# S5 output tables on SyncE's queue, and the squares of the z gates' norm in a ring of their own

## The chip, the cores and the metric

The kernel runs on one core of a Trainium2 chip. The metric is the device time of one execution in microseconds, the median of several. Engine names in the rows: PE is TensorE's matmuls, PEld its weight loads, DVE is VectorE, ACT is ScalarE, POOL is GpSimd, SP is SyncE. A name with a q behind it (SPq, ACTq) is that engine's sequencer, where transfers are issued.

## What is computed

One inference step of a decoder with two layers, for 512 prompt tokens and 64 sample tokens (576 columns together), all in fp32. Each layer has a token mixer with three branches on the same input, then a channel mixer.

```python
gates, u, q, k, v, fg, z, xbc, dt_raw = jnp.split(h @ p['w_in'][l], _in_split_points(), axis=-1)
...
y_s5, s5_re, s5_im = s5_branch(u, ...)
...
    y_fox = fox_prompt(q, k, v, logf)
...
y_ssd, conv_new, ssd_new = ssd_branch(z, xbc, dt_raw, ...)
merged = (gates[:, :, 0] * (y_s5 @ p['w_branch_s5'][l])
          + gates[:, :, 1] * (y_fox @ p['w_branch_fox'][l])
          + gates[:, :, 2] * (y_ssd @ p['w_branch_ssd'][l]))
out = merged @ p['w_o'][l]
```

The S5 branch is a complex diagonal state-space scan whose output goes through a gelu and a gated linear unit (GLU). FoX is an attention with forget gates. SSD is a chunked state-space scan whose output is multiplied by silu(z) and divided by its root mean square:

```python
y = y.reshape(bsz, seq, SSD_WIDTH) * jax.nn.silu(z.astype(jnp.float32))
y = y * lax.rsqrt(jnp.mean(jnp.square(y), axis=-1, keepdims=True) + RMS_EPS) * norm_w.astype(jnp.float32)
```

The channel mixer is a dense SwiGLU in layer 0 and a top-2-of-8 expert SwiGLU in layer 1.

## The kernel before, in words

Activations lie with channels on partitions and the 576 tokens in the free dimension, in two halves of 288. A dense projection goes by blocks of 128 output columns. `wload` (line 265) loads one block of weights, 512 KB, through SP's queue into a tile wr (three buffers). `wsplit` makes two parts of it, a rounded high part on ACT (line 97) and the rest on DVE (line 106), into wh and wl (four buffers each, two to a block of eight k-tiles). `mm3` (lines 294 to 296) then makes three matmuls for each of eight k-tiles and two halves: 48 to a block. Two PSUM banks (tag mm) hold the halves.

The order of the work: the kernel is written under a scheduler that orders each engine's instructions by a simulated time, with earlier written work first, and gives buffers out as they come free. SP is taken out of this (`manual_schedule` for SP): its queue is issued in the order in which the program is written.

`mixer(l)` is written in this order: the convolution and SSD's inputs (`conv`), `ssd`, `kqv_fox`, `s5_scan_and_out`, `fox_sample`, `fillers`, `s5_glu`, one z block, `merge5`. `kqv_fox` loads and multiplies twelve blocks (k, q and v for four pairs of heads, evacuated at line 850) and runs the prompt attention in small steps: scores (line 907), a softmax (lines 908 to 915), transposes (line 232) and the product with v (line 930). `fillers` are dense blocks with no tie to the branches: eight gate blocks in either layer (line 1337) and three z blocks (line 1344).

`s5_scan_and_out(l)` multiplies the inputs by tables (line 549), scans along time with small DVE products (lines 100, 103, 106 with tiles V and st), and swaps halves (tile vx). Its last loop goes over four groups q. For each it loads tables from DRAM: eight transfers tu of 64 KB (line 621) and a cu, in four transfers for odd q (line 627) or two for even q (line 632). All are issued by ACT. tu and the odd cu take the tag T, with three buffers in the mixer's phase, which `ssd_sample` uses for the four state tiles h0s (loaded at line 1147, stored at line 1315). The even cu takes the tag A. Lines 641 and 642 multiply tu by the inputs uc and cu by the scanned states, and the result yg passes a gelu, goes through DRAM (YD) and becomes the GLU's input.

`gate_z` is called in `merge` after its first block. It multiplies y by silu(z), squares each of four tiles on ACT (line 1258), adds them up on POOL (line 1260 and the helper at line 103), sums over partitions with a matmul by ones (line 1263), and takes the root and the reciprocal (rs, lines 1265 and 1266). Squares and rs take the tag SQ, three buffers in the phase of the mixer's end. In layer 0 that tag also holds halves of spilled gates, loaded from GD at line 1386; line 1382 loads the S5 part of the merge through POOL's queue. The work ring h288 (four buffers of one half) exists throughout, and holds z and GLU tiles in the mixer and selection tiles in routing.

Of the kernel before, what the change touches and what calls it, by code (L numbers as in the profile page):

```python
# [8 lines left out]
F32 = mybir.dt.float32  # L9
# [10 lines left out]
P = 128  # L20
# [4 lines left out]
HF = T // 2  # L25
# [20 lines left out]
def decoder_step(ctx, tc, A, O):  # L46
    nc = tc.nc
    act, dve, pool, pe, sp = nc.scalar, nc.vector, nc.gpsimd, nc.tensor, nc.sync
    consts = ctx.enter_context(tc.tile_pool(name="consts", bufs=1))
    wk = ctx.enter_context(tc.tile_pool(name="wk", bufs=2))  # L50
# [9 lines left out]
    def U(tag, shape, dt=F32, name="u"):  # L60
        return cur["pool"].tile(shape, dt, name=name, tag=tag, bufs=cur["bufs"][tag])

    def UA(shape, dt=F32, name="u"):
        return U("A", shape, dt, name)
# [19 lines left out]
    def PX(name="px"):  # L84
        return ps.tile([P, 512], F32, name=name, tag="px", bufs=2)
# [7 lines left out]
    def P5(name="p5"):  # L93
        return ps.tile([P, 512], F32, name=name, tag="p5", bufs=1)

    def cp(out, in_):
        return act.activation(out, in_, AF.Copy)  # L97

    def mul(e, out, a, b):
        return e.tensor_tensor(out, a, b, op=OP.mult)  # L100

    def add(e, out, a, b):
        e.tensor_tensor(out, a, b, op=OP.add)  # L103
# [4 lines left out]
    def stt(out, a, s, b, op0, op1):  # L108
        dve.scalar_tensor_tensor(out, a, s, b, op0=op0, op1=op1)  # L109
# [410 lines left out]
    def s5_scan_and_out(l):  # L520
# [97 lines left out]
        for q in range(4):  # L618
            tus = U("T", [P, 8, P], name="tu")
            for s in range(8):  # L620
                act.dma_start(out=tus[s * 16:(s + 1) * 16],
                              in_=KZ[l][q, :, (1 + s) * 16:(1 + s) * 16 + P].rearrange("(g c) t -> c g t", c=16))
            if q % 2:
                cu = U("T", [P, 8, P], name="cu").rearrange("p (a g) t -> p a g t", a=2)
                for i in range(2):
                    for a in range(2):
                        act.dma_start(out=cu[i * 64:i * 64 + 64, a],
                                      in_=CD[l][a * 64:a * 64 + 64, i, q * 4:q * 4 + 4, 16:144])
            else:
                cu = UA([P, 2, 4, 144], name="cu")  # L630
                for i in range(2):
                    act.dma_start(out=cu[i * 64:i * 64 + 64],
                                  in_=CD[l][:, i, q * 4:q * 4 + 4].rearrange("(a n) g t -> n a g t", a=2))
                cu = cu[:, :, :, 16:144]
            for a in range(2):
                tu = tus[:, a:8:2]
                pt = P5()
                pv = pt[:, :288].rearrange("p (g k) -> p g k", g=4)
                for g in range(4):
                    gp = q * 4 + g  # L640
                    pe.matmul(pv[:, g, :], lhsT=tu[:, g, :], rhs=uc[a][:, gp, :], start=True, stop=False)
                    pe.matmul(pv[:, g, :], lhsT=cu[:, a, g], rhs=vs[a][:, gp, 0:72], start=False, stop=True)
                yv = yg[a][:, q * 4:q * 4 + 4, :]
                y2v = [wk.tile([P, HF], F32, name="ygl", tag="v288", bufs=4).rearrange("p (g k) -> p g k", g=4)
                       for i in range(2)]
                cp(yv, pv)
                mul(dve, y2v[0], yv, yv)
                dve.tensor_scalar(y2v[0], y2v[0], 0.044715, 1.0, op0=OP.mult, op1=OP.add)
                mul(dve, y2v[0], y2v[0], yv)
                act.activation(y2v[1], y2v[0], AF.Tanh, scale=math.sqrt(2.0 / math.pi))  # L650
                stt(yv, y2v[1], 1.0, yv, OP.add, OP.mult)
# [39 lines left out]
    def YV(h, l_):  # L691
        return (V2(h), V2(l_))
# [54 lines left out]
    def mixer(l):  # L747
# [62 lines left out]
        ssd(l)  # L810
        kqv_fox(l, w_in)
        sg = s5_scan_and_out(l)
        fox_sample(l)
        fillers(l)
# [426 lines left out]
    def gate_z(l, w_in):  # L1241
        pr = prm[l]
        y2 = [U("M", [P, 2, T], name=f"y2{i}") for i in range(2)]
        zs = [U("M", [P, 2, T], name=f"zs{i}") for i in range(2)]
        for j in range(4):
            pool.dma_start(out=y2[j // 2][:, j % 2], in_=YS[l][j])
        for j in range(4):
            pool.dma_start(out=zs[j // 2][:, j % 2], in_=ZD[l][j])
        yh = [U("C", [P, 2, T], F32R, name=f"ysh{i}") for i in range(2)]
        yl = [U("C", [P, 2, T], F32R, name=f"ysl{i}") for i in range(2)]  # L1250
        for h in range(2):
            pt = PX()
            s2 = U("L", [P, HF], F32, name="lns2")
            for j in range(4):
                y_ = y2[j // 2][:, j % 2, HS[h]]
                mul(dve, y_, y_, zs[j // 2][:, j % 2, HS[h]])
                sq = U("SQ", [P, HF], F32, name="sq")
                act.activation(sq, y_, AF.Square)
                if j == 0:
                    pool.tensor_copy(s2, sq)  # L1260
                else:
                    add(pool, s2, s2, sq)
            pe.matmul(pt[:, :HF], lhsT=ones, rhs=s2, start=True, stop=True)
            rs = U("SQ", [P, HF], F32, name="rs")
            act.activation(rs, pt[:, :HF], AF.Sqrt, scale=0.25 / 512, bias=eps[:, 0:1])
            dve.reciprocal(rs, rs)
            for j in range(4):
                y_ = y2[j // 2][:, j % 2, HS[h]]
                mul(dve, y_, y_, rs)
                nw = pr[:, R_NW + j:R_NW + j + 1]  # L1270
                act.activation(yh[j // 2][:, j % 2, HS[h]], y_, AF.Copy, scale=nw)
                stt(yl[j // 2][:, j % 2, HS[h]], y_, nw, yh[j // 2][:, j % 2, HS[h]].bitcast(F32), OP.mult, OP.subtract)
        return YV(yh, yl)
# [95 lines left out]
    def merge(l, yf, mhl):  # L1369
# [10 lines left out]
        def front(j):  # L1380
            m5 = wk.tile([P, T], F32, name="m5", tag="xp", bufs=4)
            pool.dma_start(out=m5, in_=MD[l][j])
            if 1 in SPILL[l]:
                t = gtile(("XS", "SQ"))
                for h in range(2):
                    pool.dma_start(out=t[h], in_=GD[l][8 + j, :, HS[h]])
            else:
                gates(GLEAD)
                t = ready.pop((1, j))
            t = gated(l, 1, j, yf, t)  # L1390
            if j == 0:
                with tc.issue_after(S["mm"].ins):
                    ys.append(gate_z(l, A["w_in"][l]))
            for h in range(2):
                add(dve, m5[:, HS[h]], m5[:, HS[h]], t[h])
            return m5
# [641 lines left out]
```

## Time and profile before

| | us |
|---|---|
| median of 3 runs | 2404.74 |
| lowest and highest | 2397.31, 2407.87 |
| the profiled execution: its own time | 2400.34 |
| the profiled execution: span from first to last instruction | 2398.7 |
| mean granted TensorE clock over the span (1 is full) | 0.968 |

The rows further down come from the profiled execution. A row of a group of instructions gives the line, the engine, the operation, output and inputs by their names in the program, the shapes, the count, the busy time and the mean of one, and the idle time ahead of them with what ended it. Matmuls are pipelined, so their busy times overlap; how fast they really follow each other is read from their count in a stretch.

### The profile page before, as it was taken

How to read it: one execution, taken by the hardware profiler on the slowest of the kernel's cores; microseconds unless marked ns; L12 is line 12 of the kernel's file. 1: busy time of each engine (PE TensorE's matmuls, PEld its weight loads, DVE VectorE, ACT ScalarE, POOL GpSimd, SP SyncE). 2: the span in 40 equal slices, each digit the busy share in tenths (PEclk: the TensorE clock that was granted, in tenths of full speed). 3: DMA queues.
4: the chain of work that ended last, by engine and by line, in shares of the span. 5: the costliest groups of instructions: out<-in, count | busy, mean ns of one | idle time of the engine just before them, and what ended most of it. 6: DMA issues, size and time to landing. Idle time of an engine off the chain costs nothing. (4 is left out here: it accounts for less than half of the span.)

```text
span 2398.7 us, 45369 instructions
## 1 busy us (share of the span) xinstructions
PE 2277.4 (95%) x17037; PEld 2158.2 (90%) x17038; DVE 1573.7 (66%) x3725; ACT 1134.5 (47%) x2538; POOL 560.4 (23%) x712
## 2 busy tenths in 40 slices
PE   5999999998999999999999999899999699999995
PEld 5899997888998999999899998789999599999995
DVE  4956687556588843334765697456447578888886
ACT  2354443453346323223644443354334467777773
POOL 6733224333130110001124324233003310101000
PEclk7999999999999999999999999899999799999997
DMA  5566556856445432233576557757333799999993
GB/s 125 174 177 206 160 155 186 202 160 215 118 126 157 147 96 83 80 89 103 139 188 184 157 152 195 186 156 211 89 99 108 199 229 255 255 253 259 236 258 100
DMA packets 587436, 399.91 MB, mean 167 GB/s; under 512 B 59436, under 2 KB 548188, under 8 KB 587176
## 3 DMA queue, kind: packets, MB, share of 16 engines
q1 hardware_dynamic: 475272, 236.30, 37.2%
q0 software_dynamic: 30912, 95.12, 14.4%
q10 hardware_dynamic: 81024, 65.51, 9.5%
q8 instruction: 136, 2.23, 0.4%
q14 instruction: 92, 0.75, 0.1%
HBM read 326.02 MB, written 70.92 MB: 165 GB/s over the span
## 5 line engine op out<-in xcount | busy, mean ns | idle before, releaser
L106 DVE TENSOR_TENSOR wl<-wr,wh 128x512 fp32r<-128x512 f32 x886 | 629.1, 719 | 364.0 <-ACT wh L97 346.6
L97 ACT ACTIVATE wh<-wr 128x512 fp32r<-128x512 f32 x886 | 549.0, 625 | 511.0 <-PE mm L295 364.9
L294 PE MATMUL mm<-xh,wh 128*128 128x288 f32 (+1 forms) x2048 | 617.8, 302 | 15.3 <-issue 7.9
L295 PE MATMUL mm<-xl,wh 128*128 128x288 f32 (+1 forms) x2048 | 613.9, 300 | 7.9 <-issue 5.2
L296 PE MATMUL mm<-xh,wl 128*128 128x288 f32 (+1 forms) x2048 | 612.8, 299 | 5.1 <-issue 4.4
L294 PEld LDWEIGHTS mm<-xh,wh 128*128 128x128 f32 (+1 forms) x2048 | 386.3, 189 | 26.0 <-issue 11.6
L295 PEld LDWEIGHTS mm<-xl,wh 128*128 128x128 f32 (+1 forms) x2048 | 386.1, 189 | 17.1 <-issue 10.9
L296 PEld LDWEIGHTS mm<-xh,wl 128*128 128x128 f32 (+1 forms) x2048 | 385.8, 188 | 13.1 <-issue 9.8
L1788 PE MATMUL mm<-xe,wh 128*128 128x352 f32 x448 | 134.3, 360 | 1.8 <-issue 1.8
L1788 PE MATMUL pf<-xe,wh 128*128 128x352 f32 x448 | 132.2, 358 | 0.5 <-issue 0.5
L1789 PE MATMUL mm<-xe,wl 128*128 128x176 f32 x512 | 118.0, 251 | 1.8 <-issue 1.8
L1789 PE MATMUL pf<-xe,wl 128*128 128x176 f32 x512 | 117.6, 250 | 1.5 <-issue 1.5
L294 PE MATMUL mm<-hq,wh 128*128 128x288 f32 x352 | 104.3, 296 | 0.2 <-DVE rf L103 0.2
L294 PE MATMUL pf<-xh,wh 128*128 128x288 f32 x352 | 104.3, 296 | 0.0
L296 PE MATMUL mm<-hq,wl 128*128 128x288 f32 x352 | 104.2, 296 | 0.0
L296 PE MATMUL pf<-xh,wl 128*128 128x288 f32 x352 | 104.1, 296 | 0.0
L295 PE MATMUL pf<-xl,wh 128*128 128x288 f32 x352 | 103.8, 295 | 0.0
L295 PE MATMUL mm<-hq,wh 128*128 128x288 f32 x352 | 103.7, 295 | 0.0
L1789 PEld LDWEIGHTS mm<-xe,wl 128*128 128x128 f32 x512 | 97.9, 194 | 1.6 <-issue 1.6
L1789 PEld LDWEIGHTS pf<-xe,wl 128*128 128x128 f32 x512 | 97.2, 193 | 0.5 <-issue 0.5
L1788 PEld LDWEIGHTS mm<-xe,wh 128*128 128x128 f32 x448 | 86.5, 193 | 2.4 <-issue 2.4
L1337 ACT ACTIVATE gt<-mm,prm 128x288 f32<-128x288 f32 x96 | 47.4, 494 | 85.4 <-PE mm L296 75.1
(662 smaller groups left out, 5310.4 us busy)
## 6 DMA issues: line engine op xcount, KB each, us to landing
wr<-in_w_in_dram SPq DMA_DIRECT2D x108, 512.0 KB
wr<-in_moe_w_gate_dram SPq DMA_DIRECT2D x64, 512.0 KB
wr<-in_moe_w_up_dram SPq DMA_DIRECT2D x64, 512.0 KB
wr<-in_moe_w_down_dram SPq DMA_DIRECT2D x64, 512.0 KB
wr<-in_w_o_dram SPq DMA_DIRECT2D x32, 512.0 KB
wr<-in_ffn_w_gate_dram SPq DMA_DIRECT2D x25, 512.0 KB
wr<-in_ffn_w_up_dram SPq DMA_DIRECT2D x25, 512.0 KB
wr<-in_ffn_w_down_dram SPq DMA_DIRECT2D x24, 448.0 KB
```

The source lines that it names most:

```text
L97: return act.activation(out, in_, AF.Copy)
L106: e.tensor_tensor(out, a, b, op=OP.subtract)
L294: pe.matmul(o, lhsT=wh_[:, a, :m], rhs=x[0][:, k, s], start=(st and k == 0), stop=False)
L295: pe.matmul(o, lhsT=wh_[:, a, :m], rhs=x[1][:, k, s], start=False, stop=False)
L296: S["mm"] = pe.matmul(o, lhsT=wl_[:, a, :m], rhs=x[0][:, k, s], start=False, stop=(sp_ and k == kt - 1))
L1337: act.activation(t[h], o[h], AF.Tanh, scale=0.5, bias=prm[l][:, c0:c0 + 1])
L1788: pe.matmul(o, lhsT=h_[:, k % 4, :], rhs=xf, start=(k == 0), stop=False)
L1789: pe.matmul(o[:, 0:CAP], lhsT=l_[:, k % 4, :], rhs=x[:, k, 0], start=False, stop=False, skip_group_check=True)
```

## The change

The table loads of `s5_scan_and_out` are issued by SP in place of ACT, at the same place in the program. In `gate_z`, the squares and rs take buffers of the ring h288 in place of the tag SQ.

```diff
@@ -618,18 +618,18 @@
         for q in range(4):
             tus = U("T", [P, 8, P], name="tu")
             for s in range(8):
-                act.dma_start(out=tus[s * 16:(s + 1) * 16],
+                sp.dma_start(out=tus[s * 16:(s + 1) * 16],
                               in_=KZ[l][q, :, (1 + s) * 16:(1 + s) * 16 + P].rearrange("(g c) t -> c g t", c=16))
             if q % 2:
                 cu = U("T", [P, 8, P], name="cu").rearrange("p (a g) t -> p a g t", a=2)
                 for i in range(2):
                     for a in range(2):
-                        act.dma_start(out=cu[i * 64:i * 64 + 64, a],
+                        sp.dma_start(out=cu[i * 64:i * 64 + 64, a],
                                       in_=CD[l][a * 64:a * 64 + 64, i, q * 4:q * 4 + 4, 16:144])
             else:
                 cu = UA([P, 2, 4, 144], name="cu")
                 for i in range(2):
-                    act.dma_start(out=cu[i * 64:i * 64 + 64],
+                    sp.dma_start(out=cu[i * 64:i * 64 + 64],
                                   in_=CD[l][:, i, q * 4:q * 4 + 4].rearrange("(a n) g t -> n a g t", a=2))
                 cu = cu[:, :, :, 16:144]
@@ -1254,14 +1254,14 @@
             for j in range(4):
                 y_ = y2[j // 2][:, j % 2, HS[h]]
                 mul(dve, y_, y_, zs[j // 2][:, j % 2, HS[h]])
-                sq = U("SQ", [P, HF], F32, name="sq")
+                sq = wk.tile([P, HF], F32, name="sq", tag="h288", bufs=4)
                 act.activation(sq, y_, AF.Square)
                 if j == 0:
                     pool.tensor_copy(s2, sq)
                 else:
                     add(pool, s2, s2, sq)
             pe.matmul(pt[:, :HF], lhsT=ones, rhs=s2, start=True, stop=True)
-            rs = U("SQ", [P, HF], F32, name="rs")
+            rs = wk.tile([P, HF], F32, name="rs", tag="h288", bufs=4)
             act.activation(rs, pt[:, :HF], AF.Sqrt, scale=0.25 / 512, bias=eps[:, 0:1])
```

## Rows read from the trace of the kernel before

**Rows 1.** The page's busy times: us, share of the span, instructions.
```profile
PE 2277.4 (95%) x17037; PEld 2158.2 (90%) x17038; DVE 1573.7 (66%) x3725; ACT 1134.5 (47%) x2538; POOL 560.4 (23%) x712
```
**Rows 2.** Line 265 on SP's queue, 260 to 380 and 1340 to 1460; timeline between.
```profile
L265 SPq DMA_DIRECT2D wr<-in_w_in_dram x11: 367/368/368, 265.6 to 378.3; - x11
...
393.81 61.63 SPq L265 DMA_DIRECT2D wr<-in_s_w_glu_dram  x4
...
L265 SPq DMA_DIRECT2D wr<-in_w_in_dram x11: 367/368/368, 1343.3 to 1454.9; - x11
```
**Rows 3.** Lines 621 and 627: durations (ns min/median/max), first and last start; both layers.
```profile
L621 ACTq DMA_DIRECT2D tu<-KZ x32: 309/430/1690, 396.7 to 446.3; - x32
...
L627 ACTq DMA_DIRECT2D cu<-CD x8: 580/602/664, 420.6 to 450.4; - x8
...
L621 ACTq DMA_DIRECT2D tu<-KZ x32: 309/328/1545, 1477.9 to 1526.3; - x32
...
L627 ACTq DMA_DIRECT2D cu<-CD x8: 582/616/920, 1500.7 to 1531.0; - x8
```
**Rows 4.** Tile kq on ACT, 300 to 320 and 1375 to 1392 us.
```profile
L850 ACT ACTIVATE kq<-mm x2: 411/412/412, 305.2 to 310.8; 128x288 f32<-128x288 f32 x2
...
L850 ACT ACTIVATE kq<-mm x3: 393/410/410, 1377.9 to 1388.6; 128x288 f32<-128x288 f32 x3
```
**Rows 5.** Groups by line on PE, 311 to 450 and 1389 to 1531 us.
```profile
L294 PE MATMUL mm<-xh,wh 128*128 128x288 f32 x154 | 47.3, 307 | 0.0
...
L294 PE MATMUL mm<-xh,wh 128*128 128x288 f32 x152 | 46.2, 304 | 0.0
```
**Rows 6.** Stretches: us, busy of PE, PEld, DVE, ACT, POOL (count), clock, DMA, GB/s.
```profile
320.00:388.00 68.00, 67.88 (x474) 59.33 (x472) 67.47 (x241) 27.15 (x64) 18.57 (x25) 1.00 0.54 154
388.00:450.00 62.00, 55.42 (x360) 45.73 (x359) 31.16 (x80) 20.05 (x54) 20.56 (x31) 0.92 0.87 208
1400.00:1460.00 60.00, 60.00 (x432) 54.09 (x431) 59.02 (x215) 25.34 (x61) 15.99 (x22) 1.00 0.52 138
1460.00:1531.00 71.00, 67.69 (x428) 56.65 (x427) 38.88 (x101) 24.36 (x65) 23.59 (x35) 0.90 0.78 193
```
**Rows 7.** The same view for tile mm alone: PE, PEld, DVE, ACT.
```profile
388.00:450.00 62.00, 23.81 (x132) 19.67 (x131) 0.82 (x2) 2.23 (x5) 0.92 0.87 208
540.00:560.00 20.00, 20.00 (x153) 20.00 (x152) 4.54 (x10) 0.00 (x0) 1.00 0.83 250
...
1460.00:1531.00 71.00, 22.89 (x144) 19.53 (x143) 0.46 (x1) 2.40 (x5) 0.90 0.78 193
```
**Rows 8.** Groups by line on DVE, 320 to 388 us.
```profile
L100 DVE TENSOR_TENSOR st<-a,V 128x112 f32<-128x112 f32 (+1 forms) x54 | 18.6, 369 | 0.1
L106 DVE TENSOR_TENSOR wl<-wr,wh 128x512 fp32r<-128x512 f32 x12 | 8.2, 683 | 0.0
```
**Rows 9.** Stores of h0s; from the timelines, a tu issue and its first matmul.
```profile
L1315 ACTq DMA_DIRECT2D out_dram<-h0s x4: 396/401/401, 380.3 to 418.2; - x4
...
402.37 0.31 ACTq L621 DMA_DIRECT2D tu<-KZ  x1
...
408.38 0.41 PE L641 MATMUL p<-uc,tu 128*128 128x72 f32 x2 [3.09 <-DMA out_dram<-h0s]
```
**Rows 10.** Groups by line on PE, 450 to 500 us: FoX after the last table.
```profile
L930 PE MATMUL pf<-pT,vt 128*64 128x128 f32 x36 | 5.4, 282 | 0.8 <-ACT pT L97 0.8
...
L232 PE MATMUL pf<-ident,s 128*128 128x128 f32 x20 | 3.6, 278 | 0.4 <-DVE s L109 0.4
```
**Rows 11.** Timelines of ACT and POOL in `gate_z` of layer 0; PE's waits, 560 to 600.
```profile
569.40 0.44 ACT L1258 ACTIVATE sq<-y 128x288 f32<-128x288 f32 x1
...
575.76 0.43 ACT L1258 ACTIVATE sq<-y 128x288 f32<-128x288 f32 x1
...
575.57 0.54 POOL L1382 DMA_DIRECT2D m<-MD  x1 [7.04 <-DVE yfl L106]
...
PE px L1263 <- POOL lns L103: 4.1, 1, 4.1
```

## The prediction

> **What bounds the kernel now.** I read the page first: TensorE is busy for 95% of the span and no other engine for more than 66% [rows 1]. So a change pays or costs by the idle time that it takes from TensorE or gives it. Next I asked what the edited lines stand beside. The table loads of lines 621, 627 and 632 lie in the second half of each mixer, so I read SP's queue there. In layer 0 it issues eleven w_in loads between 265.6 and 378.3 us, then four for the S5 GLU; in layer 1 eleven between 1343.3 and 1454.9 us [rows 2]. By the program these are the eight gate blocks and three z blocks of `fillers`, in exactly the order in which they are written: SP's queue is issued in program order, since only SP is under the manual schedule. The ACT queue is not: its table loads, written ahead of `fillers`, run from 396.7 to 450.4 us in layer 0 and from 1477.9 to 1531.0 us in layer 1, long after the filler loads have gone out [rows 2, 3].
>
> Then I asked what TensorE lives on. The copies of the last V block end k, q and v at about 311 us in layer 0 and 1389 us in layer 1 [rows 4]. From there to the last table load, line 294 issues 154 and 152 matmuls [rows 5]; lines 295 and 296 belong to the same products, so some 462 and 456 in all. In a stretch with nothing else, 153 of them take 20 us, 0.131 us each [rows 7]. So 60.5 and 59.7 us of TensorE's work there is filler. The rest is three chains of small steps: SSD, FoX and the S5 scan. They cannot run ahead at will: from 320 to 388 us VectorE is busy 67.47 of 68 us and from 1400 to 1460 us 59.02 of 60, most of it the scan's small products (line 100 alone 18.6 us) [rows 6, 8].
>
> **The first edit: tables on SP.** Each layer issues 32 tu loads and 12 cu loads. They leave ACT and stand in SP's queue where the program has them: behind the last load of `kqv_fox` and ahead of the eleven filler loads. Nothing is computed differently. What changes is who stands behind a wait. tu and the odd cu take the tag T, three buffers that the SSD's h0s hold; these are stored from 380.3 to 418.2 us [rows 9], and only then do the first slots come free. Even with all three slots free, the tu of q = 2 takes the buffer of q = 0, which line 641 reads only after the scan; its first matmul starts at 408.38 us [rows 9]. So SP must stand still until the third and fourth groups can be issued, and behind it wait the fillers, then the GLU loads, the last z block and the w_branch loads. ACT's splits wait for these loads, and TensorE for the splits.
>
> The terms, for both layers:
> - **Cover lost.** No filler matmul can run before the last table is issued: 60.5 + 59.7 = 120.2 us of work that today lies under the chains moves behind them.
> - **Chains faster.** Without fillers the chains have the engines to themselves. In the stretch that VectorE bounds, the splits of fillers go: 12 of line 106, 8.2 us in layer 0 [rows 8], and I take the same for layer 1. In the second stretch, 388 to 450 us, fillers take 132 x 0.131 = 17.3 us and TensorE idles 62 - 55.42 = 6.6 us; in layer 1 144 x 0.131 = 18.9 and 71 - 67.69 = 3.3 us [rows 6, 7]. Chains made of waits get only part of that back: bounds nothing and all, 23.9 and 22.2 us; I take half, since ACT also loses its table issues (32 x 0.430 + 12 x 0.602 = 21 us in layer 0, 32 x 0.328 + 12 x 0.616 = 18 us in layer 1 [rows 3]). Together -(8.2 + 11.9) - (8.2 + 11.1) = -39.4 us; bounds 0 and -62.5.
> - **Work pulled forward.** FoX steps that today run after the last table can fill the hole: 5.4 + 3.6 = 9.0 us in layer 0 after 450 us [rows 10], the same taken for layer 1: -18 us; bounds 0 and -18.
> - **Restart.** When SP is free, TensorE waits for the first load and its split: from a last tu issue at 402.37 to its matmul at 408.38 us are 6.0 us [rows 9], and a split adds one pass of VectorE (0.68 us [rows 8]) and about as much of ACT: 7.3 us, twice, 14.6 us.
> - **Clock.** In the second stretches the granted clock already stands at 0.92 and 0.90 [rows 6], a mix of the 2.4 GHz and the 1.2 GHz level, where TensorE works in pieces. That is worth 0.08 x 62 + 0.10 x 71 = 12.1 us today. Without fillers the work is sparser, so I add as much again: +12.1. No row shows such a hole, so the bounds are wide: 0, and half of the other matmuls' time there (62 - 6.6 - 17.3 = 38.1 and 71 - 3.3 - 18.9 = 48.8 us), 44 us.
>
> **The second edit: a ring for the squares.** In `gate_z` of layer 0 the tag SQ (three buffers) also holds gate halves loaded from GD. The second square ends near 569.8 us, the third starts at 575.76; meanwhile POOL, which adds them up, stood 7.04 us in a load at line 1382 [rows 11]. TensorE waits 4.1 us for that sum at line 1263 [rows 11]. With four buffers of h288, unused in this phase until routing, the squares run ahead and the sum of the second half is ready sooner. POOL's stall stays. I take -5 us for both layers; bounds -10 (the clock's recovery with it) and 0, as no new wait can come from buffers that are free.
>
> **Sum.** 120.2 - 39.4 - 18.0 + 14.6 + 12.1 - 5.0 = +84.5 us on the profiled execution's own 2400.34 us, which is 0.2% under the median of 2404.74: 2485 us, 3.5% slower. All bounds at their best give 120.2 - 62.5 - 18.0 + 14.6 - 10 = +44 us, 2445; all at their worst 120.2 + 14.6 + 44 = +179 us, 2579.
>
> **Rule against row.** The rows show that the moved loads change place against the weight loads, not only their issuer [rows 2, 3]; the sum goes by that. The Trainium skill, "DMA: Bandwidth & Descriptors", section "Issuing engines are not separate DMA queues", says that loads started from sync, scalar or gpsimd share the same 16 DMA engines and that another issuer only saves the sequencer's issue time. By that rule alone the move would be worth ACT's issue time and no more, the third rival below.
>
> **Rivals.**
> *SP is not held (faster).* If SP's queue could pass the table loads, fillers would still start at 265 us, and the tables would land without ACT's delays. TensorE's idle time in the second stretches would go (6.6 + 3.3 us), with the clock's 12.1 us and the ring's 5: 2400.3 - 27 = 2373 us. It decides if the tables' buffers are free before the last k, q, v block is used up, at 311 and 1389 us. Against it: the eleven loads in written order [rows 2], h0s stored only from 380.3 us on and line 641 at 408.38 [rows 9]. Chance 0.08.
> *The chains close up (no change).* If SSD, FoX and scan without fillers ran as fast as TensorE can take them, the hole would hold little idle time, and restart less ring would be left: +14.6 - 5.0, 2410 us. For it: TensorE has 72 us of other work there (139 - 60.5 - 6.6). Against: VectorE's full 68 us, of which fillers make only 8.2 [rows 6, 8]. Chance 0.05.
> *Only issue time moves (no change).* ACT is busy 20.05 of 62 us in the second stretch [rows 6], so freeing its queue is worth at most TensorE's idle time there, 6.6 + 3.3 us, and the ring 5: 2385 us or, where ACT was not the cause, 2400. It is what the Trainium skill's rule above gives. Chance 0.03.
>
> **How the numbers follow.** A measurement of this kernel can tell about 0.5% from no change, 12 us. The forecast, SP held by the tables, has the remaining 0.84. Slower takes that and 0.01 of the closed-up chains that end just beyond the mark; the other rivals split: 0.08 for faster, 0.07 for the same. The range runs from 2430, where chains close up further than my best bounds (more of FoX's sample part pulled forward), to 2555, short of all bounds at their worst at once. What lies outside are the rivals and some 0.04 on top.
>
> **What would show it.** In the changed kernel SP's queue should show 44 table issues between the last k, q, v load and the first filler load, and filler loads starting near 430 and 1510 us of chain time instead of 265 and 1343. TensorE's idle time should lie between the last V copy and the first gate copy, some 35 to 45 us a layer, with waits that end at a split or at chain steps, and a lower granted clock there. ACT should lose the issues of lines 621 to 632. If filler loads still start before the tables, the first edit was mis-read; if the hole is there but TensorE stays over 90% busy in it, the chains closed up; if line 1263 still waits 4 us, the ring did nothing.

## Result and profile after

The changed kernel takes 2490.36 us (median of 4 runs, 2488.98 to 2492.37), the kernel before 2402.34 us beside it (4 runs): ratio 1.037, 95% interval 1.0349 to 1.0391. The forecast was 2485 us, slower. The profiled execution took 2490.47 us, its span is 2488.8 us at a mean granted clock of 0.951, against 2398.7 us at 0.968.

First the page's busy times, which answer [rows 1]: the same number of matmuls, but 34.7 us more of TensorE's time, and a smaller share of a longer span.

```profile
PE 2312.1 (93%) x17037; PEld 2177.2 (87%) x17038; DVE 1570.7 (63%) x3725; ACT 1139.7 (46%) x2538; POOL 549.6 (22%) x712
```

The timeline of SP's queue (start, us, engine, line, operation, tile, count) from 240 to 520 us answers [rows 2, 3].

```profile
249.90 9.08 SPq L265 DMA_DIRECT2D wr<-in_w_in_dram  x2
385.40 3.66 SPq L621 DMA_DIRECT2D tu<-KZ  x8
...
449.09 2.56 SPq L627 DMA_DIRECT2D cu<-CD  x4
451.75 62.02 SPq L265 DMA_DIRECT2D wr<-in_w_in_dram  x9
```

And SP's waits from 240 to 700 us (total, times, longest):

```profile
SPq L621 <- DMA out_dram<-h0s: 130.2, 3, 126.3
SPq L621 <- PE p L642: 25.1, 2, 23.0
```

SP issues the last k, q, v loads by 259 us (249.90 + 9.08) and then stands in one wait of 126.3 us for the store of h0s, whose buffer the first tu takes. Later it stands 23.0 us for the matmuls of line 642 that read an earlier group's tables. The first filler load goes out at 451.75 us; before, the eleven went out from 265.6 us on [rows 2].

What TensorE gets from that is in the stretch between the last v copy and the last table, which answers [rows 5 to 7]. The first row is the kernel before, 311 to 450 us, the second the changed kernel over the same 139 us, both with all tiles (columns as in [rows 6]); the third is tile mm alone in the changed kernel, 320 to 460 us.

```profile
311.00:450.00 139.00, 132.30 (x922) 113.20 (x921) 104.44 (x335) 52.54 (x133) 43.72 (x63) 0.96 0.71 180
...
312.00:451.00 139.00, 103.50 (x567) 72.70 (x565) 101.11 (x346) 46.23 (x129) 47.61 (x69) 0.78 0.54 139
...
320.00:460.00 140.00, 0.00 (x0) 0.00 (x0) 0.00 (x0) 0.00 (x0) 0.78 0.56 145
```

No filler matmul for 140 us, TensorE busy for 103.5 us instead of 132.3, and a granted clock of 0.78 instead of 0.96. The clock is a mix of the 2.4 GHz and the 1.2 GHz level. The chains are no shorter for it: the last table is issued at 451.0 us, against 450.4 [rows 3].

To see where the 90 us came in, I cut both traces near the same events: shortly after the start of FoX in each mixer (its first score matmul, line 907, starts at 245.8 and 1323.1 us before, at 246.8 and 1374.3 us after), and at the first (layer 0) or last (layer 1) matmul of line 1263. Before:

```profile
250.00:583.00 333.00, 323.59 (x2540) 286.57 (x2539) 218.38 (x591) 146.78 (x356) 107.33 (x152) 0.98 0.68 187
583.00:1330.00 747.00, 730.16 (x5439) 714.20 (x5438) 443.94 (x972) 304.43 (x622) 112.50 (x153) 0.98 0.44 125
1330.00:1676.50 346.50, 333.99 (x2570) 296.65 (x2569) 223.42 (x583) 154.25 (x367) 115.20 (x155) 0.97 0.65 178
```

After:

```profile
250.00:642.70 392.70, 348.81 (x2570) 302.56 (x2569) 224.04 (x601) 149.62 (x357) 107.05 (x158) 0.92 0.58 162
642.70:1380.00 737.30, 723.11 (x5408) 707.62 (x5407) 439.66 (x963) 304.16 (x620) 109.31 (x146) 0.99 0.44 125
1380.00:1768.00 388.00, 351.12 (x2579) 306.75 (x2578) 225.42 (x587) 156.27 (x367) 113.14 (x157) 0.90 0.59 160
```

Layer 0's mixer is 59.7 us longer, layer 1's 41.5; the middle is 9.7 and the rest 1.4 us shorter: 90.1 in all. Of the 59.7, 34.5 are idle time of TensorE (392.7 - 348.81 against 333 - 323.59) and 25.2 longer busy time for nearly the same matmuls (30 more of 2540); of the 41.5, 24.4 and 17.1. So of 101.2 us in the two mixers 58.9 are idleness; 42.3 are matmuls that take longer, by the lower clock or by standing apart in the pipeline, which the busy time does not tell apart. Cut exactly from line 907's first matmul to line 1263's first, the two mixers are 58.9 and 39.5 us longer, with again 59 us of idle time and 39 us of busy time.

The ring did move a wait. TensorE's waits from 560 to 670 us in the changed kernel, against [rows 11]:

```profile
PE mm L294 <- ACT ysh L1271: 5.6, 2, 4.0
...
633.68 0.54 POOL L1382 DMA_DIRECT2D m<-MD  x1 [7.61 <-DVE yfl L106]
```

Line 1263 no longer waits for POOL's sum. The next matmuls, which read the product ysh, wait for 5.6 us in its place, and POOL stands 7.61 us ahead of a load of line 1382, for the tile yfl, as before (7.04 us). (The second line is from POOL's timeline.)

### The profile page after: what moved, and what is told of

It is laid out like the page before. It is cut to its first block, busy times and chain, and to the rows that moved or that the text cites. A ratio compares the mean times of both kernels' runs of the same rounds, so it can differ in the third digit from the quotient of the medians.

```text
span 2488.8 us, 45500 instructions
## 1 busy us (share of the span) xinstructions
PE 2312.1 (93%) x17037; PEld 2177.2 (87%) x17038; DVE 1570.7 (63%) x3725; ACT 1139.7 (46%) x2538; POOL 549.6 (22%) x712
## 5 line engine op out<-in xcount | busy, mean ns | idle before, releaser
L295 PEld LDWEIGHTS mm<-xl,wh 128*128 128x128 f32 (+1 forms) x2048 | 386.6, 189 | 14.6 <-issue 9.0
L1788 PEld LDWEIGHTS pf<-xe,wh 128*128 128x128 f32 x448 | 85.5, 191 | 2.4 <-issue 2.4
## 6 DMA issues: line engine op xcount, KB each, us to landing
wr<-in_ffn_w_down_dram SPq DMA_DIRECT2D x24, 448.0 KB
```

Of the source, the lines that this page charges most:

```text
L295: pe.matmul(o, lhsT=wh_[:, a, :m], rhs=x[1][:, k, s], start=False, stop=False)
L1788: pe.matmul(o, lhsT=h_[:, k % 4, :], rhs=xf, start=(k == 0), stop=False)
```

## Experiments

My theory: a table load that waits for a buffer stands at the head of SP's queue, and the filler loads behind it leave the chains of the mixer without cover. I call the stretch without fillers the hole. Rivals: ACT losing the table issues is what costs; the number of loads is; of the hole, only TensorE's idle time could take up work, or none of it. Kernels measured together share runs of the kernel before on the same chip, where it took 2379 to 2383 us. The ranges in us of the first four expectations were worked out from the 2402 us of the result; they are compared by ratio.

**The tables alone.** The changed kernel, with sq and rs back in tag SQ.

```diff
-                sq = wk.tile([P, HF], F32, name="sq", tag="h288", bufs=4)
+                sq = U("SQ", [P, HF], F32, name="sq")
-            rs = wk.tile([P, HF], F32, name="rs", tag="h288", bufs=4)
+            rs = U("SQ", [P, HF], F32, name="rs")
```

> The first edit alone: table loads on SP, squares back in SQ. My theory (SP held by the tables takes the fillers' cover): all of the loss is here, 2490 to 2497 us, that is the changed kernel plus the ring's 0 to 5 us. Rival (a good part of the loss comes from the ring, whose h288 buffers or changed order delay the end of the mixer): below 2470 us.

2456.91 us against 2379.34: ratio 1.0296 (1.0247 to 1.0345). This missed my range, which is 1.036 to 1.039 as a ratio. Still, most of the loss is the tables', 78 of the 85 to 88 us that the whole change costs. The wait of line 1263 is back:

```profile
PE px L1263 <- POOL lns L103: 4.5, 1, 4.5
```

**The ring alone.** The kernel before, with the second edit only.

```diff
-                sq = U("SQ", [P, HF], F32, name="sq")
+                sq = wk.tile([P, HF], F32, name="sq", tag="h288", bufs=4)
-            rs = U("SQ", [P, HF], F32, name="rs")
+            rs = wk.tile([P, HF], F32, name="rs", tag="h288", bufs=4)
```

> The second edit alone: tables on ACT as before, squares and rs in h288. My theory: 2397 us, 5 us under the kernel before, and TensorE's wait for POOL's sum at line 1263 (4.1 us in layer 0) gone. Rival (POOL's queue sets the sum, not the buffers): no change within 0.2%, and the wait only moves to the next reader of the norm.

2380.15 us against 2379.34: ratio 0.9994 (0.9969 to 1.0018). No difference that can be told; the interval, 7 us less to 4 us more, does not exclude the 5 us of the forecast. TensorE's waits from 540 to 670 us:

```profile
PE mm L294 <- ACT ysh L1271: 5.3, 2, 4.0
```

The wait of line 1263 is gone and 5.3 us stand at line 294: what was ready sooner was not what comes last. Whether the ring costs anything together with the moved tables stays open: the whole change gave 1.0351 and 1.0364 further down, tables alone 1.0296, with intervals that overlap.

**Filler loads first.** The changed kernel, with the loads of all eleven filler blocks written ahead of the tables, on the same queue.

```diff
-        sg = s5_scan_and_out(l)
+        s5h = s5_scan_and_out(l)
+        next(s5h)
+        cols = [br_ * 1024 + j * P for br_ in SPILL[l] for j in range(8 if l or br_ else 0)] + \
+            [C_Z + j * P for j in range(4 - NZ[l])]
+        PRE.extend(wload(w_in, c, P, 8) for c in cols[:11])
+        sg = next(s5h)
...
-                w = wsplit(wload(src, c0 + j * P, P, kt), P, kt)
+                w = wsplit(PRE.pop(0) if PRE else wload(src, c0 + j * P, P, kt), P, kt)
```

(s5_scan_and_out yields once ahead of its last loop.)

> The changed kernel, with the eleven filler loads of each layer put ahead of the table loads in SP's queue; tables still on SP, ring kept, the same work. My theory (place in SP's queue is the whole cost): the hole after k, q, v closes, filler matmuls run from about 311 us, and the time is 2385 to 2415 us, about that of the kernel before. Rival (the cost is in what ACT gives up or in how SP issues 44 small loads): 2470 to 2495 us, like the changed kernel.

2368.87 us against 2379.34: ratio 0.9952 (0.9925 to 0.9979). SP's timeline:

```profile
240.65 121.31 SPq L265 DMA_DIRECT2D wr<-in_w_in_dram  x12
378.56 7.42 SPq L623 DMA_DIRECT2D tu<-KZ  x8
...
431.44 2.56 SPq L629 DMA_DIRECT2D cu<-CD  x4
434.10 7.30 SPq L265 DMA_DIRECT2D wr<-in_s_w_glu_dram  x4
```

The same 44 loads on the same queue, and the whole loss is gone; between 320 and 340 us tile mm has 99 matmuls again. So it is the order on the queue. This kernel is slightly faster than the kernel before, by about half a per cent; which part of it makes that gain was not separated.

**The last group alone.** Only the twelve loads of q = 3 on SP, the ring kept.

```diff
-                act.dma_start(out=tus[s * 16:(s + 1) * 16],
+                (act if q < 3 else sp).dma_start(out=tus[s * 16:(s + 1) * 16],
```

(and so at lines 627 and 632)

> Ring kept; of the four groups of tables only the last (q = 3, 12 of 44 loads) goes through SP, the others through ACT as before. My theory (the last table's wait decides when SP comes free, not the number of loads): nearly the whole loss, 2470 to 2495 us. Rival (the loss grows with the loads moved): 12/44 of 88 us, about 2425 us.

2464.4 us: ratio 1.0347 (1.03 to 1.0395). A quarter of the loads costs what all of them cost. SP's timeline:

```profile
231.89 9.08 SPq L265 DMA_DIRECT2D wr<-in_w_in_dram  x2
419.56 6.80 SPq L621 DMA_DIRECT2D tu<-KZ  x8
426.59 2.60 SPq L627 DMA_DIRECT2D cu<-CD  x4
429.30 89.61 SPq L265 DMA_DIRECT2D wr<-in_w_in_dram  x11
```

**The first group alone.** The same with `act if q else sp`: ten loads, whose buffers come free first.

> Only the eleven... no: only the ten table loads of the first group (eight tu, two cu of q = 0) are issued by SP; the other 34 stay on ACT, and the ring of the squares is kept. Theory (fillers are held until SP's last table load is out, and what they lose is the cover between the last k, q, v block and that time): SP comes free once the state stores give the first buffers back, near 395 to 400 us instead of 430 to 450, so filler matmuls are still missing for most of the chains' time (from 311 to about 400 us and in layer 1 from 1389 to about 1490 us); work covered again is the filler work of the last 50 us of each chain stretch, some 15 to 20 us a layer. Ratio 1.010 to 1.028, the first filler load near 400 us. Rival (the price comes from the later groups, whose buffers wait for the scan's reads): ratio 1.000 to 1.005.

2468.82 us against 2382.52: ratio 1.0348 (1.0297 to 1.0399). This missed my range: SP was free 50 us earlier than in the changed kernel, and the loss stayed. SP's timeline, then ACT's and TensorE's in layer 1:

```profile
364.89 3.67 SPq L621 DMA_DIRECT2D tu<-KZ  x8
380.25 1.31 SPq L632 DMA_DIRECT2D cu<-CD  x2
381.66 107.97 SPq L265 DMA_DIRECT2D wr<-in_w_in_dram  x11
...
1513.23 6.94 ACTq L621 DMA_DIRECT2D tu<-KZ  x1
...
1520.92 5.06 ACTq L621 DMA_DIRECT2D tu<-KZ  x2
1526.03 0.63 ACT L97 ACTIVATE wh<-wr 128x512 fp32r<-128x512 f32 x1 [5.00 <-DMA tu<-KZ]
...
1526.71 0.61 PE L294 MATMUL mm<-xh,wh 128*128 128x288 f32 x1 [15.58 <-ACT wh L97]
```

Less came back in either layer than I had forecast. In layer 0 the first matmul of line 1263 comes at 617.4 us, against 626.5 in the changed kernel beside it: 9 us came back, not 15 to 20, since the fillers now fall on the chains' last steps (the last S5 matmul, of line 642, moves from 448.0 to 462.2 us). In layer 1 the filler loads go out together with ACT's tables, one table issue takes 6.94 us where the median was 0.328 [rows 3], and a split behind them holds TensorE for 15.58 us; from FoX's first score to line 1263 that mixer is 2.2 us shorter than in the changed kernel. The profiled execution then loses 11.7 us behind line 1263 of layer 1, which no row explains; 10 us is also about what the interval leaves open. I read from it that the cover that counts lies before 390 us, where the scan fills VectorE, and that what SP can load after that is late already; no run tests this by itself.

**Four fillers first.** As "filler loads first", with `cols[:4]`.

> The changed kernel, with the loads of the first four filler blocks of each layer written ahead of the table loads on SP (three raw buffers stand ahead, so the fourth load waits for a split). Theory (each filler block whose load gets past the tables gives back its 48 matmuls x 0.131 us = 6.3 us of cover): four blocks a layer give back 25 us a layer, 50 of the about 85 to 92 us: ratio 1.012 to 1.022. Rival (any block behind the tables keeps the loss, since the chains then still end in an idle stretch and at a lower clock): ratio over 1.025. Rival (a few blocks are enough, because the rest of the hole has other work): ratio under 1.008.

2424.06 us: ratio 1.017 (1.0124 to 1.0216). Against the changed kernel beside it (2467.3) 43 us came back, where four blocks a layer make 50. This fits a cost that goes by the blocks whose loads come too late, each worth about its matmuls' time.

**Tables on POOL's queue.** `pool.dma_start` at lines 621, 627 and 632 of the changed kernel.

> The changed kernel with the 44 table loads of each layer on POOL's queue in place of SP's; POOL's order is the scheduler's and not the written one, as ACT's was. Theory (the cost is the place of the tables ahead of the fillers on SP's in-order queue, not that ACT lost them): fillers load from 265 and 1343 us again; ratio 0.990 to 1.012, where POOL's own issue time for tables (about 20 us a layer of an engine that is busy for a quarter of the span) may delay chain steps. Rival (tables must be issued by ACT, or arrive late from elsewhere): ratio over 1.025.

2403.94 us: ratio 1.0085 (1.006 to 1.0109). ACT has no table to issue and most of the loss is gone, so taking them from ACT was not the cost. What is left has a hole of its own, from 440 us on, when the fillers are used up (all tiles, then mm):

```profile
440.00:460.00 20.00, 17.12 (x102) 13.67 (x102) 11.12 (x30) 7.31 (x22) 6.50 (x9) 0.66 0.69 173
...
440.00:460.00 20.00, 0.00 (x0) 0.00 (x0) 0.00 (x0) 0.00 (x0) 0.66 0.69 173
```

POOL's own steps now stand among 88 issues of some 0.53 to 0.66 us each; how much of the 0.85% is theirs was not tried.

**The changed kernel again**, beside the last three kernels and beside the next two.

> The changed kernel itself beside the other runs on one chip. The tables alone gave 1.0296 (1.0247 to 1.0345), the last group alone 1.0347, and the whole change 1.037 on another chip. If the ring adds nothing, as its own run showed, this is 1.028 to 1.040; if the ring costs something only when the fillers are late, it is over 1.040.

> The changed kernel itself, beside the two with added work on one chip: 1.033 to 1.039 as before.

2467.3 us, ratio 1.0351 (1.0304 to 1.0399), and 2466.53 us, ratio 1.0364 (1.0305 to 1.0424).

**Work that nobody needs, in the hole.** The changed kernel, plus blocks of 48 matmuls on resident data, whose result is not used.

```diff
         kqv_fox(l, w_in)
+        last = S["mm"]
         sg = s5_scan_and_out(l)
         fox_sample(l)
+        for i in range(4):
+            o = [MM()[:, :HF] for h in range(2)]
+            with tc.issue_after(last.ins):
+                for h in range(2):
+                    for k in range(24):
+                        pe.matmul(o[h], lhsT=xh[:, k % 8, :P], rhs=xh[:, k % 8, HS[h]], start=(k == 0), stop=(k == 23))
         fillers(l)
```

> The changed kernel with work added that nothing uses: in each layer four blocks of 48 matmuls on the mixer's input, which needs no load, free to run from the last k, q, v block on. 2 x 192 x 0.131 = 50 us of TensorE's work. Theory (the hole that the late fillers leave is idle time, 34.5 and 24.4 us, and chain steps that take 25.2 and 17.1 us longer at the lower granted clock): the work fits in, and brings the clock back for part of the hole: within 12 us of the changed kernel, ratio to the kernel before 1.025 to 1.042. Rival (the lower clock costs nothing, the chains' waits set the hole's length): the work fills idle time only, ratio 1.033 to 1.042, with a hole as long as before it. Rival (the hole is not free, TensorE is the bound there too): the whole 50 us are added, ratio over 1.052.

> The same with nine blocks in each layer: 2 x 432 x 0.131 = 113 us added, nearly the 120 us of cover that the fillers had been. Theory (idle and lower clock together are 101 us): the time grows by 12 to 25 us over the changed kernel, ratio 1.038 to 1.050, and the granted clock of the hole is near 1. Rival (only the idle 59 us are free): 54 us more, ratio 1.055 to 1.062. Rival (nothing is free): 113 us more, ratio over 1.075.

With four blocks 2457.91 us, ratio 1.034 (1.0282 to 1.0398): 50 us of added work cost nothing (8.6 us less than the changed kernel beside it, within the intervals). With nine, 2497.25 us, ratio 1.0486 (1.0439 to 1.0532): 113 us added cost 30.7. The 20 us stretches from 300 us on (columns as in [rows 6]), first of the changed kernel beside it, then with nine blocks:

```profile
300.00:320.00 20.00, 16.39 (x75) 10.96 (x75) 17.93 (x63) 5.83 (x18) 4.82 (x8) 0.66 0.36 98
320.00:340.00 20.00, 13.69 (x68) 10.20 (x68) 17.97 (x47) 8.15 (x22) 9.55 (x14) 0.78 0.55 143
340.00:360.00 20.00, 17.91 (x62) 11.17 (x62) 19.86 (x89) 2.38 (x7) 6.22 (x7) 0.59 0.27 75
```

```profile
300.00:320.00 20.00, 20.00 (x144) 17.93 (x142) 19.62 (x64) 4.20 (x15) 3.54 (x5) 1.00 0.38 108
320.00:340.00 20.00, 20.00 (x150) 18.47 (x149) 19.69 (x80) 4.12 (x12) 4.03 (x7) 1.00 0.27 70
340.00:360.00 20.00, 19.85 (x136) 16.74 (x135) 20.00 (x91) 4.44 (x13) 5.70 (x8) 1.00 0.18 50
```

Twice the matmuls in the same 20 us, and VectorE gets through as much or more. Without added work TensorE holds the time at a clock of 0.59 to 0.78, mostly "busy"; with it the clock is 1.00. The nine blocks found 113 - 30.7 = 82 us of room. Where it was, the two mixers tell, cut from FoX's first score to the first matmul of line 1263 (the changed kernel beside it, then nine blocks):

```profile
226.80:619.40 392.60, 355.67 (x2605) 308.09 (x2603) 226.28 (x604) 150.86 (x361) 109.11 (x160) 0.91 0.58 162
1353.50:1744.40 390.90, 347.88 (x2590) 305.75 (x2590) 222.70 (x590) 150.91 (x359) 113.66 (x156) 0.91 0.59 158
...
229.70:640.90 411.20, 394.42 (x3037) 354.14 (x3036) 229.72 (x604) 151.92 (x361) 108.29 (x160) 0.98 0.55 155
1373.10:1776.20 403.10, 390.04 (x3023) 351.25 (x3023) 227.06 (x590) 148.67 (x359) 113.50 (x156) 0.97 0.56 154
```

TensorE's idle time falls by 50 us, from 80 to 30. Its busy time grows by 81 us, where the added matmuls make 113: the other 32 us are matmuls that take less of it than before, at a clock of 0.97 and 0.98 instead of 0.91. So the rival by which only idle time is free (54 us more) falls, and so does the one by which TensorE's work simply adds up. The theory's own 12 to 25 us were a little low. The chain gains too: in layer 0 the scan, from its first product to its last write of V, takes 65.3 us instead of 89.8. But the scheduler now puts fewer of FoX's and SSD's steps into that time on VectorE (8 softmax steps of line 109 instead of 15), so that the clock's part and the order's part are not told apart.

## Why the prediction was right, and where its terms were not

- **Who stands behind the wait.** Right. SP's first table waits 126.3 us for h0s, a later one 23.0 us for line 642, and fillers load from 451.75 us on, forecast near 430 in layer 0; in layer 1 they load from 1575.18 us, where the forecast of 1510 counted chain time without layer 0's delay. "Filler loads first" is the proof: same queue, same loads, no loss.
- **Cover lost, +120.2 us.** Right: 0 filler matmuls in the stretch; and "four fillers first" gave back 43 of the 50 us that its blocks were worth.
- **Chains faster, -39.4 us, with the clock, +12.1 us.** This is the step that failed. I had them make -27.3 us; the rows give about -8. Counted from FoX's first score, the last table goes out 0.4 us earlier in layer 0 (451.0 us on the clock of the trace, 450.4 before) and some 7.7 us earlier in layer 1. I had taken the fillers' splits and half of TensorE's share of the second stretch as a gain. But VectorE, the fullest engine of the first stretch [rows 6], was not relieved: its four stretches of 20 us from 320 to 400 us sum to 72.6 us of work against 75.1, though the fillers' splits (8.2 us) are gone. And the chains' own matmuls run at a granted clock of 0.64 to 0.84 in the stretches from 320 to 440 us. The scan even ends later. First its last writes of V on VectorE (the times are first and last start), before and after; then all engines from the scan's first product to its end, before and after:

```profile
L103 DVE TENSOR_TENSOR V<-st,V x14: 259/264/279, 355.9 to 388.5; 128x112 f32<-128x112 f32 x14
L103 DVE TENSOR_TENSOR V<-st,V x14: 258/268/275, 366.7 to 404.3; 128x112 f32<-128x112 f32 x14
...
312.50:388.80 76.30, 76.18 (x548) 66.90 (x547) 72.58 (x258) 31.35 (x76) 22.89 (x34) 1.00 0.59 160
312.50:404.60 92.10, 69.63 (x345) 46.85 (x344) 81.25 (x291) 28.96 (x80) 31.82 (x46) 0.77 0.49 132
```

  During the scan VectorE works 81.25 us instead of 72.58 and idles 10.9 us instead of 3.7. In place of 12 splits it does 15 of FoX's softmax steps of line 109 instead of 9, and 16 products and sums of SSD's h0s instead of 7: work that was pulled forward and now stands between the scan's products. The swap of V and vx (lines 613 to 615), on which line 642 waits, follows on POOL, where the sample part's gathers and loads stand in between:

```profile
404.71 0.58 POOL L613 DMA_DIRECT2D vx<-V  x1
...
409.71 1.15 POOL L614 COPY vx<-V 64x1168 f32<-64x1168 f32 x1 [2.63 <-DMA kpg<-in_cache_k_dram,pgi]
...
417.82 0.58 POOL L615 DMA_DIRECT2D V<-V  x1
```

  Before, lines 613 and 615 stood at 385.96 and 394.18 us. Line 615 is thus 23.6 us later, 15.8 of it by the scan's end. A term "no work is left beside them, so they speed up" needs each engine of the chain, not TensorE alone.
- **Work pulled forward, -18.0 us.** Too small. After the last table, FoX's steps (lines 907, 930 and 232) had taken 16.3 and 11.1 us in the two layers; 5.9 and 0 are left: -21.5 us. I had counted only up to 500 us, and had left out line 907 and the sample part, whose matmuls (lines 1024 to 1033 and the transposes of kpg) take 24.8 and 28.0 us between the last table and line 1263 before, and 18.9 and 21.9 us now: 12 us. About -33, roughly, since these times overlap in the pipeline; and of this the chain above paid a part back.
- **Restart, +14.6 us.** Not shown by itself. The first filler matmul comes 11 to 12 us after the last table, more than the 7.3 forecast, but TensorE has S5, FoX and sample steps to do meanwhile. By subtraction 90.1 - (120.2 - 8 - 33) leaves about 11 us, for this and all that was not counted, the shorter middle and rest among it.
- **The ring, -5.0 us.** Not found: ratio 0.9994, and in the rows a wait of 5.3 us in place of one of 4.1. "The sum of the second half is ready sooner" was true, and nothing came of it. TensorE's next block reads ysh of the first half, which comes out of root, reciprocal and product on ACT and VectorE; in the changed kernel it starts at 649.00 us, 6.3 us behind the first half's matmul of line 1263, and TensorE stands 4.05 of them. I had not asked what it would have to do next.

So the sum came out at 84.5 against 90.1 us in the spans, with errors of +19, +5, -15 and, by subtraction, -4 us that nearly cancel. The direction and the mechanism were earned; the closeness was partly luck. Of the rivals, "SP is not held" falls by SP's rows, "the chains close up" by 58.9 us of idle time, and "only issue time moves" by the measured 1.037; that ACT's issues were not the cost is shown by the kernel with the tables on POOL. The rule that it rested on (the Trainium skill, "DMA: Bandwidth & Descriptors", section "Issuing engines are not separate DMA queues") would have made this a matter of the issue time alone. The runs do not bear that out here: the same loads, issued by the same engine, give 1.037 ahead of the filler loads and 0.9952 behind them.

## What to carry to other kernels

On a queue that is issued in written order, ask of each load not when it is needed but when its buffer comes free, and write loads that can go at once ahead of those that must wait; one waiting group of ten transfers cost as much as all 44. Work without ties is worth what it covers: when it is pushed back, count its whole time as lost, and credit a faster chain only if every engine of that chain has room and if what is pulled forward does not get in its way. A wait that vanishes from one line is a gain only if what the engine does next is not waiting too.

## What the hardware showed unexpectedly

- 50 us of useless matmuls put into the hole cost nothing, and 113 us cost 30.7: the granted clock of the first 60 us of the hole rose from 0.66, 0.78 and 0.59 to 1.00, and the chain that shares TensorE did not suffer: with 113 us the last table of layer 0 goes out 199.0 us after FoX's first score against 200.1 us without, with 50 us after 176.5 us.
- The issue of one table on ACT's queue took 6.94 us (median before 0.328 [rows 3]) when filler loads, gathers and tables were in flight together; in that kernel the stretch 1500 to 1520 us had a DMA share of 1.11. That the full transfer engines hold the issue fits the rows, but was only argued.
